# A transformer encoder block on one core: one pool of tile rings for all stages, first operands of a stage asked for within the stage before, and the last two groups of the down projection side by side

## The chip, the cores and the metric

The kernel runs on one core of a Trainium2 chip. The metric is the device time of one execution in microseconds (us); a figure for a kernel is the median of several runs. The engines have the names of the profile: PE (TensorE, matmuls), PEld (its weight loads), DVE (VectorE), ACT (ScalarE), POOL (GpSimd) and SP (SyncE, which issues the DMA transfers here). PEclk is the share of its full clock that PE was granted.

## The reference

One layer over 2048 tokens of width 1024, in fp32, and a last norm:

```python
def mixer_layer(x, ...):          # convolution heads and gated linear attention heads
    z = rms_norm(x, mix_norm) @ w_in
    ...
    return concat([y_conv, y_gla]) @ w_out
def memory_cross_attention(x, mem, ...):   # 4 heads, 256 memory tokens
    ...
def sq_relu_mlp(x, mlp_norm, w_up, w_down):
    h = rms_norm(x, mlp_norm) @ w_up       # 1024 -> 4096
    return jnp.square(jax.nn.relu(h)) @ w_down
x = x + mixer_layer(x, ...)
x = x + memory_cross_attention(x, mem, ...)
x = x + sq_relu_mlp(x, mlp_norm, w_up, w_down)
return rms_norm(x, final_norm)
```

Below, x2 is the value of x after the cross attention, held in DRAM (`x2d`, features by tokens), and zu is relu(...)², also in DRAM.

## The kernel before, in words

Every fp32 product is made of three fp32r matmuls: an operand is split in a high and a low part (`split`, L112: ACT casts the high part at L113, DVE subtracts it from the source at L114), and `mm3` (L139) accumulates high x high, high x low and low x high in PSUM. All tiles have 128 partitions. Instructions are issued per engine in program order as a scheduler lays them out; an engine whose next instruction waits holds up all that is behind it.

The stages follow each other: memory keys, input projection, convolution and linear attention (to about 860 us), output projection (to about 1100 us), cross attention in 8 blocks of 256 tokens (L918 to L947, to 1419 us), the up projection (to 2113 us) and the down projection with the final norm (to the end).

**Cross attention.** The loop over `s` keeps one block ahead: scores of block s+1, probabilities of block s (`xa_probs`), output of block s. The last block ends with `xa_last` (its matmuls stand from 1395 to 1418 us). `xa_in` loads a block and takes the sum of squares of its tokens. During the last blocks x2 of the first 1024 tokens is read back from DRAM (`prep_load`, `fold`, with the adds on POOL) for the norm of the MLP; the reciprocal square roots are laid out as `rows`. Then the pool `big` is closed (L950).

**Up projection** (pool `up`, L952). It runs for two halves `hf` of 1024 tokens; in each half over 16 pairs `f` of weight tiles. One f is a 2x2 block product done with seven products instead of eight (as in Strassen's method), each of 12 matmuls 128x512 (`product`, L1053), so 84 matmuls an f. The seven token operands of a half, X1 to X7, come from `token_side`: four quarters of x2 are loaded and normed (DVE, L1014: 4 instructions a quarter), POOL makes four sums of 128x2048 elements of them (L975 with `eng=nc.gpsimd`), and each operand is split. X1, X4 and X2 are quarters or sums that need no POOL, X5, X6, X7, X3 need a POOL sum. The seven weight operands of an f come from `weight_side(f)`: two loads of 512 KB, four DVE adds of 128x512 and splits. `weight_side(f + 1)` is asked for at the start of f. The products run in the order 1, 5, 6, 2, 7, 4, 3; their results meet in PSUM tiles px, py, pz, pw and are combined by DVE in the tiles c1, u2, c22 (L975) and squared by ACT or DVE. Product 3 is accumulated upon product 5 in pz, so it must come after the DVE add that makes c22 out of pz and c1. At f 12 of the first half the sums of squares of the second half's tokens are taken (`squares`), at f 15 its `rows`. The operands of the second half are asked for when its loop starts. Then `up` is closed (L1113).

**Down projection** (pool `dn`). 16 groups `g` of two weight tiles; `dn_load(g + 1)` (weights and the zu tiles with their splits) is asked for at the start of group g. In a group there are four blocks of 512 tokens, in each 8 feature tiles `d` of 6 matmuls; DVE adds the PSUM result to `acc` (L975), which starts as x2 and is loaded after `dn_load(0)`. In the last group each finished block has its squares taken on ACT and summed on POOL, and `final_norm` (L1144) of a block is called after the matmuls of the next one: matmuls against a column of ones, L147 on DVE, a power on POOL (L149), `to_rows` on PE (L165), 8 scales on DVE (L1151) and 8 stores. The last block is cut in two of 256 tokens.

Of the kernel before, what the change touches and what calls it, by code (L numbers as in the profile page):

```python
# [30 lines left out]
def block_kernel(ctx, tc, x, mem, wm, wv, wlg, wlog, wout, wxk, wxv, wxqT, wxo, wup, wdn,  # L31
# [3 lines left out]
    phase = ExitStack()  # L35
    big = phase.enter_context(tc.tile_pool(name="big", bufs=1))
# [3 lines left out]
    NA, NG = 25, 8  # L40
# [50 lines left out]
    rows = cpool.tile([P, 2, TB], F32, name="rows")  # L91
    nhalf = cpool.tile([P, 16], F32, name="nhalf")
# [422 lines left out]
    rmem = cpool.tile([P, NMEM], F32, name="rmem")  # L515
# [126 lines left out]

    def xa_in(s, h=None):
# [266 lines left out]

    xa_rstd(0)
# [6 lines left out]
    for s in range(NS):  # L918
        if s + 1 < NS:
# [11 lines left out]
        else:  # L931
            xa_probs(s, 0)
            xa_probs(s, 1)
            xa_last(s)
# [19 lines left out]
    def W8(*shape):

        t = up.tile([P, 2048], F32, tag="w8", name="w8", bufs=6)
        return t.rearrange("p (a b) -> p a b", a=shape[0]) if shape else t

    def C8():
        return up.tile([P, 4, TB], F32R, tag="c8", name="c8", bufs=14)  # L960

    def H8():
        return up.tile([P, 2, 1024], F32R, tag="h8", name="h8", bufs=4)

    def H4():
        return up.tile([P, 2, TB], F32R, tag="h4", name="h4", bufs=2)

    def U2():
        return up.tile([P, TB], F32, tag="u2", name="u2", bufs=6)

    def US(n):
        return up.tile([P, 16], F32, tag="us", name="us", bufs=4)[:, :n]

    def add(out, a, b, op=ALU.add, eng=nc.vector):
        eng.tensor_tensor(out=out, in0=a, in1=b, op=op)  # L975

    def quarter(b, k):

        t = W8(4, TB)
        nc.sync.dma_start(t, x2d[k * TB:(k + 1) * TB, b * TB:(b + 1) * TB].rearrange("(j p) t -> p j t", p=P))  # L980
        return t

    def squares(b):

        acc = None
        for k in range(2):
            t = quarter(b, k)
            nc.scalar.activation(t, t, AF.Square)
            add(t[:, 0:2], t[:, 0:2], t[:, 2:4], eng=nc.gpsimd)
            if acc is not None:  # L990
                add(t[:, 0:2], t[:, 0:2], acc[:, 0:2], eng=nc.gpsimd)
            acc = t
        add(acc[:, 0], acc[:, 0], acc[:, 1], eng=nc.gpsimd)
        return acc[:, 0]
# [252 lines left out]
```

## Time and profile before

| | |
|---|---|
| time, median of 3 runs | 2863.25 us (2860.94 to 2864.39) |
| the profiled execution's own time | 2863.58 us |
| its span (first to last instruction) | 2861.8 us |
| PE busy | 2688.0 us, 94% |
| PE weight loads | 2286.7 us, 80% |
| DVE busy | 1584.1 us, 55% |
| ACT busy | 844.8 us, 30% |
| POOL busy | 220.0 us, 8% |
| DMA | 108 GB/s over the span |
| mean granted PE clock | 0.97 |

The page of the profile gives busy times for each engine and cuts the span into 40 slices of 71.5 us. The trace behind it can be asked for a stretch of time (windows: busy time of each engine, the granted clock, DMA share), for an engine's instructions one after the other (timeline: start, duration, what, and in brackets the idle time just before and what ended it) and for the chain of work that ended last. An instruction written L975 is made by line 975; the tile names are those of the program.

### The profile page before, as it was taken

How to read it: one execution, taken by the hardware profiler on the slowest of the kernel's cores; microseconds unless marked ns; L12 is line 12 of the kernel's file. 1: busy time of each engine (PE TensorE's matmuls, PEld its weight loads, DVE VectorE, ACT ScalarE, POOL GpSimd, SP SyncE). 2: the span in 40 equal slices, each digit the busy share in tenths (PEclk: the TensorE clock that was granted, in tenths of full speed). 3: DMA queues.
4: the chain of work that ended last, by engine and by line, in shares of the span. 5: the costliest groups of instructions: out<-in, count | busy, mean ns of one | idle time of the engine just before them, and what ended most of it. 6: DMA issues, size and time to landing. Idle time of an engine off the chain costs nothing. (4 is left out here: it accounts for less than half of the span.)

```text
span 2861.8 us, 34708 instructions
## 1 busy us (share of the span) xinstructions
PE 2688.0 (94%) x13848; PEld 2286.7 (80%) x13848; DVE 1584.1 (55%) x2367; ACT 844.8 (30%) x1216; POOL 220.0 (8%) x157
## 2 busy tenths in 40 slices
PE   6999989988889999999869998899989999999996
PEld 6898878877777889999758877688868888888885
DVE  6413372567766544333286565856547665665655
ACT  5411162423445332222233343333322011110112
POOL 1000010302200000000220020200000000000004
PEclk9999999999999999999979998899999999999998
DMA  7412363234445441111333343333253221221203
GB/s 239 156 62 67 111 216 118 89 101 117 138 144 158 153 141 45 52 41 49 123 123 112 114 144 136 103 118 101 84 205 130 85 89 45 89 89 45 89 1 118
DMA packets 157089, 310.24 MB, mean 108 GB/s; under 512 B 14016, under 2 KB 70464, under 8 KB 151808
## 3 DMA queue, kind: packets, MB, share of 16 engines
q1 hardware_dynamic: 156928, 308.04, 32.3%
q8 instruction: 108, 1.77, 0.3%
q14 instruction: 53, 0.43, 0.1%
HBM read 219.90 MB, written 88.08 MB: 108 GB/s over the span
## 5 line engine op out<-in xcount | busy, mean ns | idle before, releaser
L1058 PE MATMUL ps<-c,h 128*128 128x512 f32 x1536 | 375.7, 400 | 49.0 <-ACT c L113 35.3
L1058 PEld LDWEIGHTS ps<-c,h 128*128 128x128 f32 x1536 | 296.4, 194 | 117.6 <-ACT c L113 37.5
L141 PE MATMUL ps<-a,a 128*128 128x512 f32 (+1 forms) x840 | 305.3, 363 | 6.7 <-DVE t L245 6.7
L142 PE MATMUL ps<-a,a 128*128 128x512 f32 (+1 forms) x840 | 304.8, 363 | 0.0
L143 PE MATMUL ps<-a,a 128*128 128x512 f32 (+1 forms) x840 | 303.7, 362 | 0.0
L1058 PE MATMUL pg<-c,h 128*128 128x512 f32 x1152 | 275.2, 392 | 6.2 <-DVE c L114 3.4
L1058 PEld LDWEIGHTS pg<-c,h 128*128 128x128 f32 x1152 | 217.4, 189 | 53.4 <-DVE c L114 4.5
L975 DVE TENSOR_TENSOR acc<-ps,acc 128x512 f32<-128x512 f32 (+1 forms) x260 | 176.5, 680 | 121.6 <-PE ps L143 121.1
L975 DVE TENSOR_TENSOR acc<-pg,acc 128x512 f32<-128x512 f32 (+1 forms) x260 | 176.6, 680 | 119.5 <-PE pg L143 117.6
L141 PE MATMUL pg<-uh,wh 128*128 128x512 f32 (+1 forms) x520 | 201.9, 389 | 11.0 <-ACT uh L113 10.2
L141 PE MATMUL ps<-uh,wh 128*128 128x512 f32 (+1 forms) x520 | 202.0, 389 | 1.0 <-DVE acc L1151 1.0
L142 PE MATMUL pg<-uh,wh 128*128 128x512 f32 (+1 forms) x520 | 201.8, 388 | 0.0
L143 PE MATMUL pg<-uh,wh 128*128 128x512 f32 (+1 forms) x520 | 201.7, 388 | 0.0
L142 PE MATMUL ps<-uh,wh 128*128 128x512 f32 (+1 forms) x520 | 201.6, 388 | 0.0
L143 PE MATMUL ps<-uh,wh 128*128 128x512 f32 (+1 forms) x520 | 201.5, 388 | 0.0
L113 ACT CAST h<-w 128x1024 fp32r<-128x1024 f32 (+1 forms) x128 | 120.7, 946 | 249.1 <-PE pg L1058 135.2
L113 ACT CAST wh<-wr 128x1024 fp32r<-128x1024 f32 x32 | 33.6, 1052 | 532.6 <-PE ps L143 503.0
L114 DVE TENSOR_TENSOR h<-w,h 128x1024 fp32r<-128x1024 f32 (+1 forms) x128 | 152.4, 1193 | 62.8 <-ACT h L113 62.8
L141 PEld LDWEIGHTS ps<-a,a 128*128 128x128 f32 x840 | 160.7, 191 | 33.0 <-DVE t L245 6.3
L143 PEld LDWEIGHTS ps<-a,a 128*128 128x128 f32 x840 | 160.8, 191 | 23.2 <-issue 0.4
L142 PEld LDWEIGHTS ps<-a,a 128*128 128x128 f32 x840 | 160.9, 192 | 22.9 <-issue 0.2
L114 DVE TENSOR_TENSOR a<-raw,a 128x1024 fp32r<-128x1024 f32 (+1 forms) x76 | 88.3, 1173 | 133.2 <-PE ps L142 73.3
(320 smaller groups left out, 5221.4 us busy)
## 6 DMA issues: line engine op xcount, KB each, us to landing
w<-in_wup SPq DMA_DIRECT2D x64, 512.0 KB, 5.1
zu<-u SPq DMA_DIRECT2D x128, 256.0 KB, 2.4
ur<-zu SPq DMA_DIRECT2D x32, 1024.0 KB, 5.9
raw<-in_wm SPq DMA_DIRECT2D x32, 512.0 KB, 4.2
wr<-in_wdn SPq DMA_DIRECT2D x32, 512.0 KB, 5.4
w<-x2d SPq DMA_DIRECT2D x12, 1024.0 KB, 6.0
a<-in_x SPq DMA_DIRECT2D x32, 256.0 KB, 6.7
gt<-zv SPq DMA_DIRECT2D x32, 256.0 KB, 3.2
```

The source lines that it names most:

```text
L113: mark["act"] = nc.scalar.copy(hi, src)
L114: nc.vector.tensor_tensor(out=lo, in0=src, in1=hi.bitcast(F32), op=ALU.subtract)
L141: nc.tensor.matmul(ps, lh, rh, start=first, stop=False)
L142: nc.tensor.matmul(ps, lh, rl, start=False, stop=False)
L143: mark["pe"] = nc.tensor.matmul(ps, ll, rh, start=False, stop=last)
L975: eng.tensor_tensor(out=out, in0=a, in1=b, op=op)
L1058: nc.tensor.matmul(ps, W[w][:, ks], X[x][:, kt], start=first and kt + w + x == 0, stop=kt == 3 and w == 1, skip_group_check=not first)
```

## The change

Seven things are changed together.

1. The pools `up` and `dn` are gone; all stages take tiles from the rings of `big`, which stays open (`a` of 128x1024 tiles grows from 25 to 28, `A4`; `g` has 8, `G4`; smaller rings `st`, `raw`, `cv`, `t2`, `gt`). An operand X now is four A4 tiles, so one half's seven operands fill all 28; those of the second half take the tiles that the products of f 15 release. In the down projection 16 A4 tiles are `acc`, and 12 hold zu operands.
2. The sums of squares for the MLP norm are taken from x2 while a block of the cross attention is still in SBUF (`sumsq`, `x2_rstd`, `x2_rows`), instead of reading x2 again.
3. The first token operands (1 and 4), their loads and norms, the POOL adds and `weight_side(0)` are asked for before `xa_last` of the last block; those of the second half at f 14 and f 15 of the first.
4. The products run in the order 1, 4, 5, 6, 2, 7, 3.
5. A POOL add of 128x2048 becomes two of 128x1024 (`both`), and weight operands other than product 1's and 2's are split in pieces of 128x512.
6. `dn_load` loads zu by halves of 1024 columns; `acc` is 16 tiles, loaded by halves.
7. The last two groups of the down projection are taken together: for each block of tokens the matmuls of both groups, then the next block. `finish` of a block (sums, power, rows, scales, stores) is laid by hand between the feature tiles of the next block on PE and DVE. The last block's squares are summed on DVE.

The core of the diff:

```diff
-    phase = ExitStack()
-    big = phase.enter_context(tc.tile_pool(name="big", bufs=1))
+    big = ctx.enter_context(tc.tile_pool(name="big", bufs=1))
-    NA, NG = 25, 8
+    NA, NG = 28, 8
...
             xa_probs(s, 1)
+            x2_rstd(s - 1)
+            sides = [token_side(0)]
+            next(sides[0])
+            X = dict([next(sides[0])])
+            W = weight_side(0, T2)
+            X.update([next(sides[0])])
             xa_last(s)
+            f_last = sumsq(live[s]["xs"])
             continue
         xa_out(s, 0)
         if s + 2 < NS:
             xa_in(s + 2)
-        else:
-            G2 = lambda: G4(F32, (P, 2, TB))
-            sq = [fold(prep_load(x2d, b, XR), G2, nc.gpsimd) for b in (0, 1)]
...
-    phase.close()
-    up = phase.enter_context(tc.tile_pool(name="up", bufs=1, reuse_waits="tile"))
...
+    def both(out, a, b, op):
+        for i in range(2):
+            add(out[i], a[i], b[i], op, nc.gpsimd)
...
+    def token_side(hf):
+        a11 = quarter(hf, 0, 0, S2())
+        a22 = quarter(hf, 1, 1, R2())
+        a21 = quarter(hf, 1, 0, S2())
+        yield None
+        yield 1, operand(a11)
+        yield 4, operand(a22)
+        s = a22
+        both(s, a21, a22, ALU.add)
+        yield 5, operand(s)
+        both(s, s, a11, ALU.subtract)
+        yield 6, operand(s)
+        both(a21, a11, a21, ALU.subtract)
+        a12 = quarter(hf, 0, 1, S2())
+        yield 2, operand(a12)
+        yield 7, operand(a21)
+        both(a12, a12, s, ALU.subtract)
+        yield 3, operand(a12)
...
-            nxt = weight_side(f + 1) if f + 1 < 16 else None
+            if f + 1 < 16:
+                nxt = weight_side(f + 1)
+            if hf == 0 and f == 14:
+                sides.append(token_side(1))
+                next(sides[1])
             product(px, W[1], x(1), True)
             nc.scalar.copy(c1, px)
+            product(pw, W[4], x(4), True)
             product(pz, W[5], x(5), True)
             product(py, W[6], x(6), True)
...
-            product(pw, W[4], x(4), True)
             add(c1, c1, pw, ALU.subtract)
             product(pz, W[3], x(3), False)
...
+            if hf == 0 and f == 15:
+                nxt = weight_side(0)
...
+    pair = [nxt, dn_load(NG_ - 1)]
+    blocks = [(0, cs) for cs in halves] + [(1, halves[0]), (1, slice(TB, TB + TH)), (1, slice(TB + TH, 2 * TB))]
+    todo = None
+    with tc.manual_schedule(engines={EngineType.PE, EngineType.DVE}):
+        for n, (c, cs) in enumerate(blocks):
+            column(*pair[0], c, cs, between=todo)
+            sq = column(*pair[1], c, cs, nc.vector if n == len(blocks) - 1 else nc.gpsimd, todo)
+            for _ in todo or ():
+                pass
+            todo = finish(c, cs, sq)
```

How the order of instructions moves is shown at three places.

DVE, in the middle of a half of the up projection, one f between its products 6 and 3. Before, `u_14724` is u2, `u_14698` is c1, `u_14755` is c22, `h` are split weight operands and `w` weight sums:

```order
L975 TENSOR_TENSOR u_14724<-pg,u_14698 128x512
L114 TENSOR_TENSOR h_14667<-w_14665,h_14667 128x1024
L114 TENSOR_TENSOR h_14668<-w_14665,h_14668 128x1024
L975 TENSOR_TENSOR w_15049<-w_15046 128x512
L975 TENSOR_TENSOR u_14698<-pg,u_14698 128x512
L975 TENSOR_TENSOR w_15049<-w_15046,w_15049 128x512
L975 TENSOR_TENSOR u_14755<-ps,u_14698 128x512
```

After, `t_15232` is u2, `t_15194` is c1, `t_15263` is c22, `g` are split weight operands and `gt` weight sums:

```order
L924 TENSOR_TENSOR t_15232<-pg,t_15194 128x512
L114 TENSOR_TENSOR g_15153<-gt,g_15152 128x512 x2
L924 TENSOR_TENSOR gt<-cv,raw 128x512
L924 TENSOR_TENSOR gt<-cv,gt 128x512
L114 TENSOR_TENSOR g_15155<-gt,g_15154 128x512 x2
L924 TENSOR_TENSOR gt<-gt,raw 128x512
L924 TENSOR_TENSOR gt<-cv 128x512
L924 TENSOR_TENSOR t_15194<-pg,t_15194 128x512
L114 TENSOR_TENSOR g_15291<-raw,g_15290 128x1024
L924 TENSOR_TENSOR t_15263<-ps,t_15194 128x512
```

All four weight sums, four splits of 128x512 and one of 128x1024 now stand between u2 and c22.

POOL, from the end of the cross attention to the first half's last operand. Before (`w` are the quarters and sums of the up projection; the row of L149 makes both `rows`):

```order
L149 TENSOR_TENSOR sm<-sm,nhalf 128x4 x2
L975 TENSOR_TENSOR w_11998<-w_11986,w_11992 128x2048
L975 TENSOR_TENSOR w_11986<-w_11962,w_11986 128x2048
L975 TENSOR_TENSOR w_11998<-w_11998,w_11962 128x2048
L975 TENSOR_TENSOR w_12035<-w_12035,w_11998 128x2048
```

After (`st`, `raw`, `cv` are the quarters and sums; the two rows of L149 are the powers of `x2_rstd` for block 6 and of the last block's sums, which follow `xa_last`):

```order
L924 TENSOR_TENSOR raw<-st,raw 128x1024
L924 TENSOR_TENSOR st<-st 128x1024
L924 TENSOR_TENSOR cv<-st,cv 128x1024
L924 TENSOR_TENSOR st<-st 128x1024
L149 TENSOR_TENSOR sm<-sm,nhalf 128x2
L924 TENSOR_TENSOR raw<-raw,st 128x1024
L924 TENSOR_TENSOR cv<-cv,st 128x1024
L149 TENSOR_TENSOR sm<-sm,nhalf 128x2
L924 TENSOR_TENSOR st<-st,raw 128x1024
L924 TENSOR_TENSOR st<-st,cv 128x1024
```

A half has eight adds instead of four, and six of them stand ahead of the power that follows `xa_last`.

PE, where the up projection ends. Before, the last product 3 (L1058 on `ps`), then the first matmuls of the down projection (L141 to L143 on `uh`, `wh`):

```order
L1058 MATMUL ps<-c_14259,h_15949 128x512 x2
L1058 MATMUL ps<-c_14260,h_15949 128x512
L1058 MATMUL ps<-c_14259,h_15949 128x512
L141 MATMUL pg<-uh,wh 128x512
L141 MATMUL ps<-uh,wh 128x512
```

After, the end of product 7 (L1009 on `pg`), eight matmuls of the down projection, and product 3 (L1009 on `ps`):

```order
L1009 MATMUL pg<-a_14533,g_16413 128x512
L141 MATMUL pg<-a_16661,g_16656 128x512
L142 MATMUL pg<-a_16662,g_16656 128x512
L143 MATMUL pg<-a_16661,g_16657 128x512
L141 MATMUL pg<-a_16673,g_16668 128x512
L142 MATMUL pg<-a_16674,g_16668 128x512
L143 MATMUL pg<-a_16673,g_16669 128x512
L141 MATMUL ps<-a_16661,g_16656 128x512
L142 MATMUL ps<-a_16662,g_16656 128x512
L1009 MATMUL ps<-a_14563,gt 128x512
```

The down projection's first matmuls thus stand ahead of the up projection's last product.

More of the change, by code (lines that the diff above doesn't have):

```diff
@@ L512, in gla_out @@
         return attn, outp, fin
-    rmem = cpool.tile([P, NMEM], F32, name="rmem")
+    rmem = rows[:, 0, :NMEM]
     memT = []
@@ L909, in block_kernel, with add, kts, operand @@
     wA = [load_w(row(zA, kt)) if kt < 6 else load_st(row(zA, kt)) for kt in range(KT)]
+    def add(out, a, b, op=ALU.add, eng=nc.vector):
+        eng.tensor_tensor(out=out, in0=a, in1=b, op=op)
+    def kts(t):
+        return [t[j // 2][:, (j % 2) * TB:(j % 2 + 1) * TB] for j in range(4)]
+    def operand(src):
+        c = [A4(F32R) for _ in range(4)]
+        for i in range(2):
+            split(src[i], c[i], c[2 + i])
+        return kts(c[:2]), kts(c[2:])
+    def S2():
+        t = ST(F32, (P, 2, 1024))
+        return [t[:, i] for i in range(2)]
@@ new lines, in product, with sq_relu @@
+    def product(ps, W, X, first):
+        for kt in range(4):
+            ks = slice(kt * P, (kt + 1) * P)
+            for w, x in ((0, 0), (0, 1), (1, 0)):
+                nc.tensor.matmul(ps, W[w][:, ks], X[x][kt], start=first and kt + w + x == 0,
+                                 stop=kt == 3 and w == 1, skip_group_check=not first)
+    def sq_relu(t, src, f, b):
+        nc.scalar.activation(t, src, AF.Relu)
+        nc.scalar.activation(t, t, AF.Square)
+        nc.sync.dma_start(zu[f * P:(f + 1) * P, b * TB:(b + 1) * TB], t)
@@ L968, in U2 @@
[L968 to L994, printed above, removed]
@@ L1053, in product @@
-    def product(ps, W, X, first):
-        for kt in range(4):
-            ks = slice(kt * P, (kt + 1) * P)
-            for w, x in ((0, 0), (0, 1), (1, 0)):
-                nc.tensor.matmul(ps, W[w][:, ks], X[x][:, kt], start=first and kt + w + x == 0,
-                                 stop=kt == 3 and w == 1, skip_group_check=not first)
-    def sq_relu(t, src, f, b):
-        nc.scalar.activation(t, src, AF.Relu)
-        nc.scalar.activation(t, t, AF.Square)
-        nc.sync.dma_start(zu[f * P:(f + 1) * P, b * TB:(b + 1) * TB], t)
@@ new lines, in finish @@
+    def finish(c, cs, sq):
+        for _ in range(3):
+            yield
+        rc = final_sums(sq, cs.stop - cs.start, PS)
+        yield
+        yield
+        r = to_rows(rc, PG)
+        for d in range(KT):
+            final_scale(c, cs, r, d)
+            yield
+    NG_ = FF // P // G
+    halves = [slice(0, TB), slice(TB, 2 * TB)]
+    for g in range(NG_ - 2):
+        (us, ws), nxt = nxt, dn_load(g + 1)
+        for c in range(2):
+            for cs in halves:
+                column(us, ws, c, cs)
@@ new lines, in block_kernel @@
+    pair = [nxt, dn_load(NG_ - 1)]
[8 more added lines that the diff above has]
+            todo = finish(c, cs, sq)
+        for _ in todo:
+            pass
```

258 lines of the change are left out of this document (111 added, 147 removed).

## The prediction

> **What bounds the kernel now.** I read the page first:
>
> ```profile
> span 2861.8 us, 34708 instructions
> PE 2688.0 (94%) x13848; PEld 2286.7 (80%) x13848; DVE 1584.1 (55%) x2367; ACT 844.8 (30%) x1216; POOL 220.0 (8%) x157
> PE   6999989988889999999869998899989999999996
> PEclk9999999999999999999979998899999999999998
> ```
>
> PE is busy 94% of the span, so nothing but PE's own holes can be won. In its row the dips from the middle on are slices 21 (a 6, with the clock at 7), 25 and 26 (8, clock 8), 30 (8) and the last (6, clock 8). They are the openings of the up projection's two halves, that of the down projection, and the end of the kernel. Sums by windows size them; the columns are busy time of PE, PEld, DVE, ACT, POOL, then granted clock, DMA share and GB/s:
>
> ```profile
> 1150.00:1395.00 245.00, 243.96 (x1607) 222.97 (x1606) 90.35 (x208) 63.26 (x150) 22.49 (x15) 1.00 0.18 57
> 1395.00:1419.00 24.00, 23.47 (x196) 23.21 (x193) 3.79 (x10) 1.23 (x3) 0.00 (x0) 1.00 0.03 9
> 1419.00:1441.00 22.00, 0.47 (x1) 0.29 (x1) 15.83 (x22) 7.12 (x7) 0.00 (x0) 0.58 0.90 325
> 1441.00:1480.00 39.00, 25.52 (x79) 18.14 (x79) 32.13 (x18) 14.82 (x11) 20.57 (x4) 0.75 0.10 34
> 1771.00:1784.00 13.00, 7.09 (x35) 6.51 (x34) 7.13 (x13) 3.54 (x4) 2.87 (x2) 0.62 0.64 234
> 1784.00:1828.00 44.00, 29.33 (x88) 21.14 (x89) 36.62 (x22) 14.86 (x12) 20.60 (x4) 0.73 0.09 30
> 2113.00:2124.00 11.00, 0.79 (x3) 0.40 (x2) 3.03 (x4) 2.54 (x3) 0.00 (x0) 0.61 0.80 285
> 2124.00:2131.00 7.00, 6.96 (x20) 5.03 (x20) 5.44 (x5) 3.44 (x4) 0.00 (x0) 0.63 1.01 421
> 2131.00:2780.00 649.00, 649.00 (x2865) 537.39 (x2864) 421.17 (x570) 87.24 (x90) 0.00 (x0) 1.00 0.23 83
> ```
>
> The row 2131:2780 gives the price of one 128x512 matmul at full clock: 649 / 2865 = 0.2265 us. The timeline of PE gives the same (one f is 84 matmuls, from 1516.77 to 1535.81, 19.04 us or 0.2267 each) and shows the holes:
>
> ```profile
> 1440.53 0.79 PE L1058 MATMUL ps<-c,h 128*128 128x512 f32 x1 [22.06 <-ACT c L113]
> 1452.91 2.50 PE L1058 MATMUL ps<-c,h 128*128 128x512 f32 x5 [5.58 <-ACT c L113]
> 1516.77 8.32 PE L1058 MATMUL ps<-c,h 128*128 128x512 f32 x36
> 1535.81 8.32 PE L1058 MATMUL ps<-c,h 128*128 128x512 f32 x36
> 1690.85 10.08 PE L1058 MATMUL ps<-c,h 128*128 128x512 f32 x36 [2.56 <-DVE u L975]
> 2110.51 2.88 PE L1058 MATMUL ps<-c,h 128*128 128x512 f32 x12
> 2123.60 0.79 PE L141 MATMUL pg<-uh,wh 128*128 128x512 f32 x1 [10.21 <-ACT uh L113]
> 2127.16 0.63 PE L142 MATMUL pg<-uh,wh 128*128 128x512 f32 x1
> 2127.59 0.63 PE L143 MATMUL pg<-uh,wh 128*128 128x512 f32 x1
> ```
>
> What each hole holds beyond its matmuls:
>
> - Opening 1, 1419 to 1480: 61 us for 80 matmuls, 61 - 80 x 0.2267 = **42.9**. First 22 us of nothing (loads, norms, first split: the pool had just been closed), then waits for operands.
> - A stall at 1690: 2.56 idle, and the 36 matmuls behind it take 10.08 instead of 8.32: **4.3**. It stands where the second half's squares are taken.
> - Opening 2, 1771 to 1828: 57 us for 88 products of 0.2267 and 0.4 us of small ones: 57 - 20.4 = **36.6**.
> - Opening 3, 2113.2 (2110.51 + 12 x 0.2267) to 2131: 17.8 us for 23 matmuls, 17.8 - 5.2 = **12.6**.
> - The down projection from 2131 to the end of the span: 730.8 us. All of it is 16 x 192 x 0.2267 = 696.4, of which 23 matmuls are counted above: 730.8 - 691.2 = **39.6**, nearly all after 2780.
>
> That is 136.0 us in five places, and the change touches all five.
>
> **Why an operand takes so long to make.** In opening 1 POOL and DVE stand like this:
>
> ```profile
> 1440.51 2.29 DVE L114 TENSOR_TENSOR c<-w,c 128x2048 fp32r<-128x2048 f32 x1
> 1452.89 4.79 DVE L114 TENSOR_TENSOR c<-w,c 128x2048 fp32r<-128x2048 f32 x1 [6.78 <-ACT c L113]
> 1457.60 7.02 DVE L1014 SCALAR_TENSOR_TENSOR w<-w,vec,rows 128x512 f32<-128x512 f32 x4
> 1550.70 1.22 DVE L114 TENSOR_TENSOR h<-w,h 128x1024 fp32r<-128x1024 f32 x1 [1.49 <-ACT h L113]
> ```
>
> ```profile
> 1446.42 9.11 POOL L975 TENSOR_TENSOR w<-w,w 128x2048 f32<-128x2048 f32 x2 [52.51 <-DVE w L1014]
> 1457.76 4.99 POOL L975 TENSOR_TENSOR w<-w,w 128x2048 f32<-128x2048 f32 x1 [2.23 <-DVE c L114]
> ```
>
> The last DVE row, from the middle of the half, is a split of 128x1024: 1.22. The split of 128x2048 takes 2.29 us alone and 4.79 when it starts at 1452.89 within a POOL add, and the four norms that run into POOL's add at 1457.76 take 7.02. So a POOL add and a DVE instruction with two SBUF inputs do not run together: the later one waits. [...] What the change can do about it is only to put the adds elsewhere and to halve their length.
>
> **The change, part by part.**
>
> *Opening 1.* The 22 us go: loads, norms and the operands of products 1 and 4 lie within the cross attention, where DVE has room (3.79 of 24 us in 1395:1419). Cover: `xa_last`, 23 us of matmuls in that row. But two costs take their place. First, the new work stands on ACT, DVE and POOL ahead of the last block's probabilities; a weight load that waits for its ring slot, two casts and a POOL lock of half an add (4.5 us for 128x2048 by 9.11 / 2, so 2.3) delay `xa_last` by about 3 to 5. Second, products 1 and 4 of f 0 and product 1 of f 1 give PE only 36 x 0.2267 = 8.2 us before X5, X6, X2, X7 are needed, each of which wants a POOL add or a norm behind POOL, casts and two splits of about 1.15. Before, from the first product (1440.5) to full rate (1480) 39.5 us held 18 of matmuls, 21 lost; six of eight adds now lie earlier, so I take 13 of these and 2 to 3 of half clock after a stall. Left: 4 + 13 + 2.5 = 19.5 of 42.9, **gain 23**. Bounds: the 22 less 5 of `xa_last`'s delay and 5 of new waits, 12; all hidden but 4 of that delay and 2.9 of clock, 36.
>
> *Stall at 1690.* The reads and POOL adds behind it are gone: -4.3. `x2_rows` and `x2_rstd` in its place cost some small matmuls, about 1.3. **Gain 3** (0 to 4.3).
>
> *Opening 2.* The 13 us of `rows` at its head go (done at f 12), and loads and norms are done during f 14. But all 28 A4 tiles hold the first half's operands: X1 of the second can be split only when product 1 of f 15 is over, and so on in turn, and X5 needs four tiles behind product 5. Each split is behind POOL's add and behind product 7's results on DVE's one queue, in 19 us of f 15. DVE has in that f its usual work of 10.7 us (seven combining steps and four weight sums of 0.6, splits of 1.1 + 5 x 0.6), 14 splits of 128x1024 at 1.15 are 16 us more and POOL's adds 8 x 2.3 = 18 lock against these. That can't end in 19 us: 10.7 + 16 + part of 18 is 30 to 40. I take 20 left of 36.6, **gain 16** (8, the 13 less 5 of new waits, to 30, where only 6.6 is left).
>
> *Opening 3.* `dn_load(0)` takes tiles that product 1 and 4 of the last f release, 14 us before its end, and eight matmuls of the down projection stand ahead of product 3. `acc` needs its first tile after 1.4 us and is loaded behind product 5's release. About 0.6 left, **gain 12** (8 to 12.6).
>
> *Tail.* The end now, and the sums and rows on PE from the chain:
>
> ```profile
> 2842.65 4.74 POOL L975 TENSOR_TENSOR q<-q 128x256 f32<-128x256 f32 x6 [6.30 <-ACT q L1175]
> 2847.35 0.71 POOL L149 TENSOR_TENSOR ds<-ds,nhalf 128x2 f32<-128x2 f32 x1
> 2852.81 0.71 POOL L149 TENSOR_TENSOR ds<-ds,nhalf 128x2 f32<-128x2 f32 x1 [4.06 <-DVE ds L147]
> 2843.30 0.42 DVE L975 TENSOR_TENSOR acc<-ps,acc 128x256 f32<-128x256 f32 x1
> 2854.90 3.22 DVE L1151 SCALAR_TENSOR_TENSOR acc<-acc,vec,ps 128x256 f32<-128x256 f32 x8 [2.17 <-PE ps L165]
> ```
>
> ```profile
> 2834.91 1.37 PE ps L165 x8
> 2853.57 1.23 PE ps L165 x4
> ```
>
> Blocks finish one 512-block of matmuls apart now, 96 x 0.2267 = 21.8 us, instead of 10.9, so a block's POOL sums and scales (13 us) fit under the next block. After the last matmul: an add, a square and two sums on DVE (0.42 each), sums on PE and L147 0.5, power 0.71, rows 1.2, scales 3.22, and 3.7 from the last scale (2858.1) to the span's end: 11. Before it, final sums and rows of four blocks on PE, 1.4 each by the row of L165 at 2834.91, 5.6, and stalls between blocks about 4. Left 20.6 of 39.6, **gain 19** (13 to 24).
>
> *Steady state.* This goes the other way. Before, product 3 began 0.4 us after c22 and never waited:
>
> ```profile
> 1546.95 0.69 DVE L975 TENSOR_TENSOR u<-pg,u 128x512 f32<-128x512 f32 x1 [6.20 <-issue]
> 1549.61 1.05 ACT L113 CAST h<-w 128x1024 fp32r<-128x1024 f32 x1 [1.66 <-PE ps L1058]
> 1553.17 0.68 DVE L975 TENSOR_TENSOR w<-w,w 128x512 f32<-128x512 f32 x1
> 1553.77 0.68 DVE L975 TENSOR_TENSOR u<-ps,u 128x512 f32<-128x512 f32 x1
> 1554.85 5.38 PE L1058 MATMUL ps<-c,h 128*128 128x512 f32 x23
> ```
>
> Now product 4 no longer stands between 7 and 3; product 1 of the next f and one matmul do, so 37 x 0.2267 = 8.4 us lie between the end of product 6 and product 3. DVE has behind u2 eleven more instructions up to c22 itself, 0.60 apart (1.13 behind the split of 128x1024), and the cast before that split (1.05) waits for product 7, which ends 5.4 us in. u2 starts 0.26 in: 0.26 + 9 x 0.6 = 5.7, with waits for two casts 6.0, c1 to 6.6, the split to 7.8, c22 to 8.5. That is 0.1 late; with the error of such a sum 0 to 0.25 each f, for 30 f's **a loss of 4** (0 to 8). The queue waits only for itself; what is behind it is DVE's next f, with 8 us to spare.
>
> *Ahead of the up projection.* Squares of x2 (2 casts' worth of ACT, about 3 us of DVE a block) lie beside PE (DVE 90 of 245 us there), and three more A4 tiles let loads start earlier: 0 (-4 to +4).
>
> **Sum.** 23 + 3 + 16 + 12 + 19 - 4 = 69. The profiled execution took 2863.58, 0.33 above the median and 1.8 more than its span, so about 2863.5 - 69 = **2794**.
>
> The half clock after a stall is in the traces: PEclk 0.58 to 0.75 in the openings, and 0.43 us a matmul. [...]
>
> **Rivals.**
>
> (a) *The openings only move.* POOL's lock and the chain add, cast, split, matmul stay as they are, and the added work delays `xa_last` and f 15 by what is saved. For it: POOL's 20.6 us in each opening are the same elements; the A4 ring is full. Against: 22 us of opening 1 wait for loads and norms alone. Then only opening 3, the tail, the stall and the loss count: 12 + 19 + 3 - 4 = 30, 2833. Chance 0.15.
>
> (b) *The openings vanish.* Operands are ready in time but for some 5 us each: gains 37 and 31, and no loss in the steady state: 37 + 31 + 3 + 12 + 19 = 102, 2761. For it: DVE is busy 57% in the steady f (10.7 of 19). Against: f 15's sum above. Chance 0.15.
>
> (c) *Slower: product 3 waits on DVE's queue in every f.* The place is c22, eleventh behind u2. If one of the casts before it waits for a later product than I read (the `g` ring has eight tiles for six an f), c22 comes late by a cast and the splits behind it: product 7 instead of product 2 for the second pair of splits makes 5.7, cast 0.6, two splits 1.2, two sums 1.2, c1 0.6, split 1.1 and c22 0.7, together 11.1, which is 2.7 late, 30 x 2.7 = 81 lost instead of 4: 2863.5 - 73 + 81 = 2872. It decides from 73 / 30 = 2.4 us an f. Against: the tiles come free in turn, and the product that I read is 2, one before 7. Chance 0.04, a further 0.02 for a loss that just eats the gain.
>
> (d) *The scheduler undoes it*: the prefetches are placed behind `xa_last`'s work anyway. The order shows them ahead, so this counts within (a).
>
> The forecast has 0.64. 0.2% of the time, 5.7 us, is about what a measurement of this kernel can tell from no change. Range: the forecast's terms in quadrature (12, 12, 6, 4, 4) give about 19, or 25 for eight times in ten; up to 2832 it takes in most of (a), down to 2764 part of (b): 2764 to 2832. Faster 0.94, same 0.02, slower 0.04.
>
> **What would show it.** Right: the first 22 us hole gone with X1's product right behind `xa_last`; PE waits of 1 to 6 us for ACT or DVE in openings 1 and 2, POOL's adds beside long splits; no 10 us hole before the down projection; some 20 us less at the end; gaps of 0.1 to 0.2 before product 3 in each f. Wrong: `xa_last` later by more than 8, opening 2 over 30 or under 8, or a pitch of an f over 19.3.

## The result, and the profile after

The changed kernel takes **2796.05 us** (median of four runs, 2792.35 to 2800.03); the kernel before, run beside it, 2862.58. The ratio is 0.9768, interval 0.9751 to 0.9785: 2.3% faster, 66.5 us. The prediction was 2794.0 in 2764 to 2832. The profiled execution took 2798.06 us with a span of 2795.9, 65.9 less than the span before. One execution of a later repeat of this kernel (e9 below) took 6807.44 us; e9's median counts it (2789.53 without it), its ratio does not. The page of the profile:

```profile
span 2795.9 us, 35187 instructions
PE 2677.4 (96%) x13896; PEld 2281.7 (82%) x13896; DVE 1613.2 (58%) x2504; ACT 859.2 (31%) x1298; POOL 190.4 (7%) x146
PE   7999989988889999999989999899999999999998
PEclk8999999999999999999999999899999999999999
```

PE is busy 10.6 us less although it has 48 matmuls more, since fewer of them run at half clock: the mean granted clock is 0.98 instead of 0.97, and over opening 1, as defined below, 0.95 (1402.2 to 1501.92) instead of 0.85 (1395.1 to 1516.77). The other 55 us are idle time that went. Slice 21 went from 6 to 8 and its clock from 7 to 9, one 8 is left of slices 25 and 26, slice 30 is a 9, and the last slice went from 6 to 8.

*The openings.* PE's timeline around the end of `xa_last` (L1009 is the product's line now, `a` the token operand, `g` or `gt` the weight operand), then product 3 in f 2, f 11 to f 14 and the second f of the second half:

```profile
1432.32 2.91 PE L1009 MATMUL ps<-a,g 128*128 128x512 f32 x12
1435.40 5.73 PE L1009 MATMUL ps<-a,g 128*128 128x512 f32 x24 [0.17 <-ACT a L113]
1445.20 0.61 PE L157 MATMUL pg<-vec,t 128*128 128x1 f32 x4 [4.07 <-DVE t L651]
1460.57 1.66 PE L1009 MATMUL pg<-a,g 128*128 128x512 f32 x6 [1.35 <-DVE a L114]
1463.90 1.89 PE L1009 MATMUL pg<-a,g 128*128 128x512 f32 x7 [1.67 <-DVE a L114]
...
1501.92 3.03 PE L1009 MATMUL ps<-a,gt 128*128 128x512 f32 x12
...
1674.43 3.00 PE L1009 MATMUL ps<-a,gt 128*128 128x512 f32 x12
1693.58 2.99 PE L1009 MATMUL ps<-a,gt 128*128 128x512 f32 x12
1714.54 3.03 PE L1009 MATMUL ps<-a,gt 128*128 128x512 f32 x12
1733.73 3.00 PE L1009 MATMUL ps<-a,gt 128*128 128x512 f32 x12
...
1810.02 3.00 PE L1009 MATMUL ps<-a,gt 128*128 128x512 f32 x12
```

The hole of 22 us is gone: product 1 starts where `xa_last` ends. To compare kernels I measure both openings in one way. Opening 1 runs from the last transpose of the probabilities to product 3 of f 2, opening 2 from product 3 of f 14 to product 3 of the second half's second f; the matmuls between (at 0.12 and 0.2267 us) are subtracted. Before, the transposes ended at 1395.1 and product 3 of f 2 began at 1516.77: 121.7 - 192 x 0.12 - 240 x 0.2267 = 44.2 beyond the matmuls. After, 1402.2 to 1501.92, with 253 instead of 240 matmuls, is 99.7 - 80.4 = 19.3. Opening 2 was 94.2 - 57.1 = 37.1 and is 1810.02 - 1733.73 - 57.1 = 19.2. In the steady part nine f's lie between 1501.92 and 1674.43: 19.17 each, where it was 19.04. The `rows` of the second half are 16 small matmuls on PE just ahead of 1693.58; the two f's around them, from 1674.43 to 1714.54, take 40.11, which is 1.8 more than two steady ones.

*What holds PE in opening 2.* In order: POOL's sums (L924), DVE's queue, PE.

```profile
1740.21 3.38 POOL L924 TENSOR_TENSOR raw<-st,raw 128x1024 f32<-128x1024 f32 x1 [277.45 <-DVE a L114]
1743.67 2.40 POOL L924 TENSOR_TENSOR st<-st 128x1024 f32<-128x1024 f32 x1
1746.03 3.32 POOL L924 TENSOR_TENSOR cv<-st,cv 128x1024 f32<-128x1024 f32 x1
```

```profile
1744.71 2.44 DVE L114 TENSOR_TENSOR a<-raw,a 128x1024 fp32r<-128x1024 f32 x1 [3.37 <-ACT a L113]
1750.47 2.40 DVE L114 TENSOR_TENSOR a<-cv,a 128x1024 fp32r<-128x1024 f32 x1 [3.31 <-ACT a L113]
1752.79 0.68 DVE L924 TENSOR_TENSOR t<-pg,t 128x512 f32<-128x512 f32 x1
1753.39 5.05 DVE L114 TENSOR_TENSOR g<-gt,g 128x512 fp32r<-128x512 f32 x2
```

```profile
1753.52 4.41 PE L1009 MATMUL pg<-a,g 128*128 128x512 f32 x12 [6.15 <-DVE t L924]
1764.38 5.49 PE L1009 MATMUL ps<-a,gt 128*128 128x512 f32 x12 [3.05 <-DVE t L924]
1784.27 4.38 PE L1009 MATMUL pg<-a,g 128*128 128x512 f32 x12 [3.55 <-DVE t L924]
```

This is one chain, read from the bottom. PE waits 6.15 us for the combining step at 1752.79, which takes 0.68 and would have been possible long before; but it is queued on DVE behind the split at 1750.47, which waits 3.31 for ACT's cast, and the cast waits for POOL's sum that ends at 1749.4. The splits take 2.4 instead of 1.22, and two of 128x512 take 5.05 where 1.3 is usual, while POOL's adds run on to 1757.90. In these rows a split and an add of POOL hold each other up. The split begun at 1744.71, within POOL's add of 1743.67 to 1746.07, takes 2.44 and ends 1.08 us after that add; POOL's next add, begun at 1746.03 within this split, takes 3.32 instead of 2.40. The combining step at 1752.79, which has one input in PSUM, keeps its 0.68 although a POOL add runs from 1751.75 to 1755.10. What these rows show is called the lock below, as in the prediction. PE's three waits are 12.75 us, and the 12 matmuls behind each take 1.5, 2.6 and 1.5 more than the 2.88 of full clock: 18.4 of the 19.2.

*Opening 3 and the tail.* PE at the start of the down projection, then DVE at the end:

```profile
2072.60 2.88 PE L1009 MATMUL pg<-a,g 128*128 128x512 f32 x12
2075.32 0.39 PE L141 MATMUL pg<-a,g 128*128 128x512 f32 x1
2077.13 2.90 PE L1009 MATMUL ps<-a,gt 128*128 128x512 f32 x12
2079.87 0.39 PE L143 MATMUL ps<-a,g 128*128 128x512 f32 x1
```

```profile
2787.06 0.16 DVE L147 TENSOR_SCALAR sm<-ps 128x2 f32<-128x2 f32 x1 [0.70 <-PE ps L1138]
2789.31 3.22 DVE L1143 SCALAR_TENSOR_TENSOR a<-a,vec,pg 128x256 f32<-128x256 f32 x8 [2.09 <-PE pg L165]
```

The first matmul of the down projection follows product 7 (L1009 on `pg`) without a gap, where 12.6 us stood. From 2075.32 to the end are 720.6 us; without product 3 (2.7) and the 696.4 of matmuls 21.5 are left of 39.6.

### The profile page after: what moved, and what is told of

It reads as the page before. It is cut to its first block, busy times and chain, and to the rows that moved or that the text cites. A ratio compares the mean times of both kernels' runs of the same rounds, so it can differ in the third digit from the quotient of the medians.

```text
span 2795.9 us, 35187 instructions
## 1 busy us (share of the span) xinstructions
PE 2677.4 (96%) x13896; PEld 2281.7 (82%) x13896; DVE 1613.2 (58%) x2504; ACT 859.2 (31%) x1298; POOL 190.4 (7%) x146
## 5 line engine op out<-in xcount | busy, mean ns | idle before, releaser
L141 PE MATMUL ps<-a,a 128*128 128x512 f32 (+1 forms) x840 | 307.1, 366 | 6.8 <-DVE t L245 6.8
L143 PE MATMUL ps<-a,a 128*128 128x512 f32 (+1 forms) x840 | 306.5, 365 | 0.0
L1009 PE MATMUL pg<-a,g 128*128 128x512 f32 x1152 | 287.0, 394 | 13.1 <-DVE t L924 9.7
L1009 PE MATMUL ps<-a,g 128*128 128x512 f32 x1152 | 277.5, 389 | 0.2 <-ACT a L113 0.2
L1009 PEld LDWEIGHTS pg<-a,g 128*128 128x128 f32 x1152 | 219.3, 191 | 61.4 <-DVE t L924 6.6
L141 PE MATMUL ps<-a,g 128*128 128x512 f32 (+1 forms) x672 | 260.0, 387 | 0.0
L143 PE MATMUL ps<-a,g 128*128 128x512 f32 (+1 forms) x672 | 258.3, 384 | 0.0
L142 PE MATMUL ps<-a,g 128*128 128x512 f32 (+1 forms) x672 | 258.2, 384 | 0.0
L1009 PEld LDWEIGHTS ps<-a,g 128*128 128x128 f32 x1152 | 216.0, 188 | 45.4 <-ACT a L113 0.6
L924 DVE TENSOR_TENSOR a<-ps,a 128x512 f32<-128x512 f32 (+1 forms) x264 | 178.0, 674 | 121.4 <-PE ps L143 120.0
L924 DVE TENSOR_TENSOR a<-pg,a 128x512 f32<-128x512 f32 (+1 forms) x264 | 177.9, 674 | 115.7 <-PE pg L143 115.6
L113 ACT CAST g<-raw 128x1024 fp32r<-128x1024 f32 (+3 forms) x118 | 114.9, 983 | 360.7 <-issue 237.6
L141 PE MATMUL pg<-a,g 128*128 128x512 f32 (+1 forms) x528 | 202.7, 384 | 0.0
L143 PE MATMUL pg<-a,g 128*128 128x512 f32 (+1 forms) x528 | 202.0, 383 | 0.0
L142 PE MATMUL pg<-a,g 128*128 128x512 f32 (+1 forms) x528 | 202.0, 383 | 0.0
L141 PEld LDWEIGHTS ps<-a,a 128*128 128x128 f32 x840 | 162.8, 194 | 32.3 <-DVE t L245 4.8
L143 PEld LDWEIGHTS ps<-a,a 128*128 128x128 f32 x840 | 162.8, 194 | 23.1
L114 DVE TENSOR_TENSOR g<-raw,g 128x1024 fp32r<-128x1024 f32 (+3 forms) x118 | 137.4, 1173 | 29.8 <-ACT g L113 28.3
```

What stands on the lines that cost most here:

```text
L113: mark["act"] = nc.scalar.copy(hi, src)
L114: nc.vector.tensor_tensor(out=lo, in0=src, in1=hi.bitcast(F32), op=ALU.subtract)
L141: nc.tensor.matmul(ps, lh, rh, start=first, stop=False)
L142: nc.tensor.matmul(ps, lh, rl, start=False, stop=False)
L143: mark["pe"] = nc.tensor.matmul(ps, ll, rh, start=False, stop=last)
L1009: nc.tensor.matmul(ps, W[w][:, ks], X[x][kt], start=first and kt + w + x == 0, stop=kt == 3 and w == 1, skip_group_check=not first)
```

## The experiments

What was in dispute after the result: why 19 us are left in each opening. The first theory is the prediction's: in opening 2 DVE has more work than time, and the ring of `A4` tiles is full. The rival: POOL's token sums, through the lock with DVE and as a link of the chain. Besides, it was open which part of the change (one pool, the requests, the pair of groups) brought what. The measured numbers of all kernels stand here; openings are us beyond the matmuls, as defined above, and "down" is from the up projection's last product 3 to the end of the span.

| kernel | median us | ratio to before (interval) | opening 1 | opening 2 | down |
|---|---|---|---|---|---|
| before | 2862.58 | 1 | 44.2 | 37.1 | |
| after | 2796.05 | 0.9768 (0.9751 to 0.9785) | 19.3 | 19.2 | 718.8 |
| e9, after again | 2792.93 | 0.9755 (0.9738 to 0.9772) | 19.5 | 19.2 | 718.8 |
| e1, no requests ahead | 2805.22 | 0.9805 (0.9791 to 0.982) | 34.7 | 17.3 | 718.3 |
| e2, sums on DVE | 2762.25 | 0.9654 (0.9639 to 0.9667) | 6.3 | 2.7 | |
| e3, no pair of groups | 2800.0 | 0.9788 (0.9772 to 0.9804) | 18.8 | 19.3 | 727.0 |
| e4, weights of the output projection later | 2790.44 | 0.9756 (0.974 to 0.9773) | 18.8 | 19.3 | 718.8 |
| e5, before, sums on DVE | 2839.61 | 0.9933 (0.9915 to 0.9951) | 34.7 | 22.5 | |
| e6, after, `s` in its own tiles | 2791.13 | 0.9761 (0.9746 to 0.9775) | 22.0 | 16.4 | |
| e7, e2 with before's order of products | 2765.29 | 0.9666 (0.9648 to 0.9685) | 7.7 | 6.2 | |
| e8, e2 with idle work on POOL | 2792.34 | 0.9765 (0.9743 to 0.9787) | 26.3 | 17.9 | |
| e10, e2 and e4 | 2757.6 | 0.9634 (0.9617 to 0.965) | 6.3 | 2.7 | |
| e11, e2 and e1 | 2772.06 | 0.9689 (0.9675 to 0.9704) | 17.9 | 2.7 | |

In opening 2 of e2, e8, e10 and e11 one matmul more than 252 lies between the two product 3, and its 0.2 us are still in the figures; in e7 there are five more, and their 1.1 us are taken off. The ratios hold each kernel against runs of the kernel before that were made beside it.

**e1: the requests back at the start of each half, one pool kept.** The blocks that call `token_side` and `weight_side` within the cross attention and at f 14 and 15 are taken out; instead:

```diff
+        if hf == 0:
+            sides = []
+        X = {}
+        sides.append(token_side(hf))
+        next(sides[hf])
+        X.update([next(sides[hf])])
+        W = weight_side(0)
```

> The changed kernel, with the requests put back to the start of each half: token operands and first weight operands of a half are asked for when its loop begins, as before the change, but still in the one pool. Theory A (the one pool does the work, the requests little: the order already lays loads and norms ahead of the last block's matmuls): the last block starts some 4 to 6 us earlier, the first product of the up projection some 3 to 5 us later behind it, opening 2 within 2 us of the changed kernel; 2791 to 2801. Theory B (the requests bring the gain of the openings, 23 and 16 us): openings of 36 to 43 and 30 to 37 us again, 2815 to 2835.

Measured 2805.22, 9 us above after. Product 3 of f 2, of f 14 and of the second f of half 2:

```profile
1511.70 3.02 PE L1009 MATMUL ps<-a,gt 128*128 128x512 f32 x12
...
1743.46 3.00 PE L1009 MATMUL ps<-a,gt 128*128 128x512 f32 x12
...
1817.83 3.02 PE L1009 MATMUL ps<-a,gt 128*128 128x512 f32 x12
```

The transposes ended at 1396.6. So opening 1 is 115.1 - 80.4 = 34.7, 15 more than after; opening 2 is 74.4 - 57.1 = 17.3, no more than after. (The spans differ by 7.3 only, since e1's transposes ended 5.6 earlier; see e9.) In the second opening the requests bring nothing: what shortened it from 37.1 lies in the rest of the rewrite, which stays in e1. Its largest part can be read from the kernel before, where the `rows` of the second half and X1's first cast held up PE from 1771.5 to 1784.1, 12.6 us with 32 small matmuls; now the `rows` are made at f 12. The sums in halves and product 4 right behind product 1 were not tried one by one. In the first opening the requests bring 15, though not through loads and norms: all but the last quarter's norms end by 1381.4 in e1 as well. What stands behind the last block's work there are the casts and splits of X1 and X4, and POOL's sums behind them: X1 is split at 1425.2 instead of 1390.1, and POOL's first sum starts at 1434.7 instead of 1394.1. The hole of 22 us does not come back; PE waits 1.1 us for X1. Whether that is due to the one pool or to the norm's sums, which are now taken beforehand, no run separates.

**e2: the eight token sums of a half on DVE.** One word:

```diff
-            add(out[i], a[i], b[i], op, nc.gpsimd)
+            add(out[i], a[i], b[i], op)
```

> The changed kernel, with the token sums (eight adds of 128x1024 in each half) on DVE instead of POOL. Theory A (what is left of the openings is POOL's chain and its lock on DVE: 2.4 to 3.4 us an add on POOL, splits of 2.4 instead of 1.2 beside them): each opening 3 to 6 us shorter, 2784 to 2790. Theory B (DVE's own load is the bound there: 10.7 us of one f and 16 of splits): the adds come on top, 9 us each, 2804 to 2814.

Measured 2762.25, 34 us below after and far below both theories. The openings are 13.0 and 16.5 us shorter, 29.5 together, where theory A had 3 to 6 each; in the profiles most of the rest lies ahead of them, as e2's transposes ended 7.5 earlier (see e9). Product 3 at the same three places, and below it the sums by windows over opening 2 of after and of e2 (PE, PEld, DVE, ACT, POOL busy, then PEclk, DMA share, GB/s):

```profile
1481.35 3.00 PE L1009 MATMUL ps<-a,gt 128*128 128x512 f32 x12
...
1713.11 3.00 PE L1009 MATMUL ps<-a,gt 128*128 128x512 f32 x12
...
1772.87 2.91 PE L1009 MATMUL ps<-a,gt 128*128 128x512 f32 x12
```

```profile
1733.73:1810.02 76.29, 63.55 (x254) 51.04 (x253) 62.16 (x70) 32.80 (x47) 24.18 (x8) 0.89 0.36 111
```

```profile
1713.11:1772.87 59.76, 58.32 (x254) 47.19 (x254) 57.53 (x74) 33.28 (x47) 0.00 (x0) 1.00 0.43 137
```

DVE now has the eight sums as well, 8 x 1.22 = 9.8 us, and is busy 57.5 of 59.8 us; yet opening 2 falls from 19.2 to 2.7 and PE's clock stays at 1. So DVE's work was not too much for the time, and the full `A4` ring did not bind either: the ring is the same. The second half's 14 splits lie between 1713.0 and 1762.1 in e2, over two and a half f's and not within f 15 alone. The eight sums took POOL 24.2 us, and they made DVE's other instructions longer, as its groups in the same windows show, after and then e2:

```profile
L114 DVE TENSOR_TENSOR g<-gt,g 128x512 fp32r<-128x512 f32 x12 | 13.6, 1177 | 0.0
L114 DVE TENSOR_TENSOR a<-st,a 128x1024 fp32r<-128x1024 f32 x8 | 11.9, 1495 | 0.0
```

```profile
L114 DVE TENSOR_TENSOR a<-st,a 128x1024 fp32r<-128x1024 f32 x8 | 9.6, 1219 | 0.0
L114 DVE TENSOR_TENSOR g<-gt,g 128x512 fp32r<-128x512 f32 x12 | 7.6, 686 | 0.0
```

This leaves two readings of the gain: the lock, or only the faster sums in the chain. e8 tells them apart.

**e5: the kernel before with its four sums of 128x2048 on DVE** (`eng=nc.gpsimd` dropped in four lines).

> The kernel before, with one edit: its four token sums of 128x2048 in each half on DVE instead of POOL. Theory A (the lock between POOL and DVE also held up the openings of the kernel before, beside loads and the closed pool): each opening some 8 to 12 us shorter, 2838 to 2846. Theory B (there the loads and norms bound the openings, and the sums only mattered once these were hidden): within 5 us of 2860.

Measured 2839.61, 19.6 us below the runs of before that were made beside it (2859.23). Both openings shrink, by 9.5 and 14.6 us, but the hole ahead of the first product stays:

```profile
1441.21 0.80 PE L1058 MATMUL ps<-c,h 128*128 128x512 f32 x1 [22.27 <-ACT c L113]
```

POOL's sums were thus a cost of their own in the kernel before, beside the 22 us that the change removes, and the change left them on POOL.

**e8: e2, and POOL adds a constant to the high parts of operands 5, 6, 7 and 3,** into a scratch tile that nobody reads: 16 pieces of 128x512 a half. No operand depends on POOL's work. In opening 2 it takes more of POOL's time than the sums did, 30.1 us against 24.2, so that it shows what the lock can do, and not the exact share that it had in the change.

```diff
+            if d is not None:
+                for j in range(2):
+                    add(d, cst[:, :TB], c[i][:, j * TB:(j + 1) * TB].bitcast(F32), eng=nc.gpsimd)
```

> The kernel with the sums on DVE, and beside each of the operands 5, 6, 7 and 3 POOL adds a constant to the operand's high part, in four pieces of 128x512, into a scratch tile that nobody reads (16 pieces a half, some 20 us of POOL; no work of the reference is left out). Nothing waits for these, so only the lock between POOL and DVE can cost. Theory A (the lock is what cost the openings): 10 to 25 us slower than 2762. Theory B (the chain through the slower POOL adds is what cost): within 4 us of 2762.

Measured 2792.34: 30 of e2's 34 us are lost again. One POOL piece alone in opening 1 and the 16 of opening 2, then DVE's groups in opening 2, and a wait of PE (L1013 here is L1009 elsewhere):

```profile
1438.50 1.28 POOL L924 TENSOR_TENSOR gt<-cst,a 128x512 f32<-128x512 f32 x1
...
1761.98 31.26 POOL L924 TENSOR_TENSOR gt<-cst,a 128x512 f32<-128x512 f32 x16 [296.85 <-DVE g L114]
```

```profile
L114 DVE TENSOR_TENSOR a<-st,a 128x1024 fp32r<-128x1024 f32 x8 | 14.8, 1876 | 0.0
L114 DVE TENSOR_TENSOR g<-gt,g 128x512 fp32r<-128x512 f32 x12 | 9.8, 864 | 0.0
L959 DVE SCALAR_TENSOR_TENSOR st<-st,vec,rows 128x512 f32<-128x512 f32 x4 | 5.9, 1511 | 2.0 <-DMA st<-x2d 2.0
```

```profile
1769.83 2.93 PE L1013 MATMUL ps<-a,g 128*128 128x512 f32 x6 [3.99 <-DVE a L114]
```

No wait in opening 2 names POOL, and in opening 1 only two of DVE do, 1.0 us in all, for the power of the norm's sums and not for these pieces; PE waits for DVE's splits, which take 1.88 instead of 1.22 us in the mean. The spans differ by 30.2 us: opening 1 takes 20.0 and opening 2 15.2 more, while the work ahead of them ends 5.0 earlier. So the lock alone, with no dependence on POOL, costs the openings 35.2 us, more than the 29.5 that e2 won there. How the 29.5 divide between the lock and the slower chain through POOL's sums is not shown. The rows show both sides paying: POOL's 16 pieces take 30.1 / 16 = 1.88 instead of 1.28, too.

**e6: the first sum in tiles of its own.** In after, `s` overwrites `a22`, so POOL's first sum waits for the split of X4 (the 277 us at 1740.21 end with that split).

```diff
-        s = a22
+        s = R2()
```

> The changed kernel, sums still on POOL, but the first sum written to tiles of its own instead of over the operand of product 4, so that POOL need not wait until that operand is split into tiles that product 4 of f 15 frees. Theory A (what cost 16 us in opening 2 is when POOL's chain may start): opening 2 some 6 to 9 us shorter, 2787 to 2791. Theory B (it is the length of POOL's chain and the lock, wherever it starts): opening 2 within 3 us of 18.9, 2793 to 2799.

Measured 2791.13, within the intervals of after. POOL's first sum starts 0.6 us before product 3 of f 14 (at 1727.8) instead of 6.5 after it (at 1740.2), but opening 2 gets only 2.8 us shorter, and opening 1 gets 2.7 longer. So it is not the start of POOL's chain that holds opening 2.

**e3: the last two groups of the down projection one after the other** (the first through all four half-blocks, then the last, with `finish` still between its matmuls).

```diff
+    for c in range(2):
+        for cs in halves:
+            column(*pair[0], c, cs)
...
-            column(*pair[0], c, cs, between=todo)
```

> The changed kernel, with the last two groups of the down projection one after the other again; each block's sums, rows and scales still lie between the feature tiles of the next block, which now has 10.9 us of matmuls instead of 21.8. Theory A (the gain at the end, 18 us, comes from the pair): 12 to 18 us slower, 2808 to 2814. Theory B (it comes from the interleaving and the sums on DVE, the pair only costs buffers): within 4 us, 2792 to 2800.

Measured 2800.0 as a median, 4 us above after, not to be told apart by the intervals; but the stage itself is clear. Down takes 2797.0 - 2070.04 = 727.0 instead of 718.8, and PE waits for the power of a block's sums. Over the whole execution this is 12.2 us in six waits, 3.7 in three after; within the down projection it is 9.5 in four and 1.0 in one:

```profile
PE pg L165 <- POOL sm L149: 12.2, 6, 3.1
```

```profile
PE pg L165 <- POOL sm L149: 3.7, 3, 1.4
```

The pair is worth 8 of the 18 us that the tail became shorter. That the spans differ by 1.1 us only comes from the start of the execution: the transposes ended 6.6 us earlier than in the profile of after (see e9).

**e9: the changed kernel once more.**

> The changed kernel itself once more, beside the next two. Theory A (the wait of 4.0 us at the first sums of squares of the cross attention, which its profile showed, belongs to that one execution): the first transposes of the cross attention's probabilities start at 1078 to 1081 us instead of 1085.3, the median is 2790 to 2798. Theory B (it belongs to the change): 1084 to 1086 again.

Measured 2792.93. The transposes of the cross attention in the profile of after, and in this one:

```profile
L712 PE MATMUL pg<-cst,t x128: 271/273/302, 1085.3 to 1402.2; 128*128 128x128 f32 x128
```

```profile
L712 PE MATMUL pg<-cst,t x128: 271/272/302, 1076.7 to 1393.6; 128*128 128x128 f32 x128
```

The span is 8.5 us shorter, 2787.4, and all of it lies ahead of the first transpose, 8.6 us; the openings and the down projection are the same to 0.2. So the profile shown of after is an execution in which the early stages took long, and the 7 us by which its transposes end later than before's are no effect of the change. Over the profiles of the kernels made from the changed one the transposes end anywhere from 1389.7 (e8) to 1402.2. What in those stages varies I have not found.

**e4: six of the eight weight tiles of the output projection loaded later** (behind its last sum of the stage before), against a wait of PE at L157 near 1037 which is 4.0 us in the profile of after.

```diff
-            wO = [load_w(row(zO, kt), T=A4 if kt < 6 else G4) for kt in range(KT)]
+            wO = [load_w(row(zO, kt), T=A4 if kt < 6 else G4) for kt in range(2)]
+            with behind("y"):
+                wO += [load_w(row(zO, kt), T=A4 if kt < 6 else G4) for kt in range(2, KT)]
```

> The changed kernel, with all but two of the eight loads and splits of the cross attention's output weights laid behind the last add of the output projection. Theory A (the larger ring let a third weight split stand ahead of those adds on DVE, and PE waits 4.0 us for them and runs some us at half clock): 5 to 6 us faster, 2790 to 2791, with no wait at the first sums of squares. Theory B (the 6 us come from elsewhere, or the later weights are then missed): within 2 us of 2796 or slower.

Measured 2790.44, the number of theory A. The wait is gone, but in other executions of the kernel without the edit it is only 1.1 to 1.8, and the ratios 0.9756 and 0.9768 or 0.9755 do not differ. No effect can be shown.

**e7: e2 with before's order of products (1, 5, 6, 2, 7, 4, 3), operands in that order, `s` in its own tiles.** It tests the loss in the steady part.

> The kernel with the sums on DVE, and the order of products of the kernel before (1, 5, 6, 2, 7, 4, 3), operands made in that order too, the first sum in tiles of its own. Theory A (product 3 waits 0.13 us in each f for the sum c22, since a split of 128x1024 stands before it on DVE; with product 4 between 7 and 3 it need not): an f takes 19.04 instead of 19.17 us, and the openings lose some 1 to 3 us each, 2756 to 2763. Theory B (the longer f has another cause): 19.17 us an f still.

Measured 2765.29, no better than e2. Nine f's apart, product 3 shows the pitch, and a wait of opening 2 where the gain went:

```profile
1503.70 2.88 PE L1009 MATMUL ps<-a,gt 128*128 128x512 f32 x12
...
1675.06 2.88 PE L1009 MATMUL ps<-a,gt 128*128 128x512 f32 x12
...
1750.86 0.51 PE L1009 MATMUL ps<-a,g 128*128 128x512 f32 x1 [3.10 <-ACT a L113]
```

171.36 / 9 = 19.04: the loss of the steady part is due to the new order. But opening 2 has 6.2 instead of 2.7 left, and opening 1 7.7 instead of 6.3: product 4 no longer stands behind product 1, where its 12 matmuls gave the operands behind it 2.7 us. That reason is argued, not tried by itself. What 28 f's by 0.13 bring, 3.6, is paid in the two openings.

**e10: e2 and e4 together.**

> The kernel with the sums on DVE, and the output weights of the cross attention laid behind the last add of the output projection. Theory A (that weight split in front of the adds costs in some executions): 2756 to 2761 and a smaller spread. Theory B (it costs nothing measurable): within 3 us of 2762.

Measured 2757.6, the fastest kernel here: 0.9634 (0.9617 to 0.965). Against e2's 0.9654 the intervals overlap, so e4's part stays undecided.

**e11: e2 and e1 together,** the requests without the lock.

> The kernel with the sums on DVE, and the operands and first weights of a half asked for when its loop begins. Theory A (the request is worth the time in which X1 and X4 are split behind the last block, about 5 to 9 us, and the rest of the 15 us that it was worth with sums on POOL was the lock): 2766 to 2772. Theory B (it is worth the same 15 us without the lock): 2775 to 2780.

Measured 2772.06. Opening 1 is 17.9 instead of 6.3 us, opening 2 is 2.7 as in e2. The requests are thus worth 12 us in opening 1 (15 with the sums on POOL, e1) and nothing in opening 2, with the lock or without it.

## Why the prediction was right

By its own steps, predicted gain and measured one (us):

| step | predicted | measured | from |
|---|---|---|---|
| opening 1 | 23 | 24.9 | 44.2 to 19.3 |
| stall at 1690 | 3 | 2.5 | 4.3 to 40.11 - 2 x 19.17 |
| opening 2 | 16 | 17.9 | 37.1 to 19.2 |
| opening 3 | 12 | 12.6 | no gap left |
| tail | 19 | 18.1 | 39.6 to 21.5 |
| steady state | -4 | -3.6 | 28 x (19.17 - 19.04) |
| ahead of the up projection | 0 | -7.1 | 1395.1 to 1402.2, that execution alone |
| sum | 69 | 65.3 | the spans differ by 65.9 |

- *Opening 1* went as laid out: of the 19.3 us left, 6.8 are the delay of `xa_last` within its block (30.1 us from the last transpose to product 1, 23.3 before), where 3 to 5 were expected, and the rest new waits and half clock. POOL's sums, which the prediction charged here with their lock, are the larger part: with the sums on DVE (e2) 13.0 of the 19.3 go, 4.3 of them from the delay of `xa_last`. One wait was not foreseen: at 1445.20 PE stood 4.07 us for four small matmuls of block 7's sums, which only the second half needs; on PE's queue they stand ahead of 24 matmuls that run as soon as these four are done. In e2 the same wait is 0.82.
- *`xa_last` later by more than 8* was named as a sign against the forecast, and it did end 13.9 us later. 7.1 of these come from the early stages, and e9 shows that they are not the change's; 6.8 are. The sign was put down without a fixed start to count from.
- *Opening 2* has the predicted size, but the step that gave it is wrong in its main reason. The prediction added DVE's 10.7 and 16 us to part of POOL's 18 and said that this can't end in 19 us. e2 gives DVE 9.8 us more and opening 2 is nearly gone. What holds it is the third item of that sum: the adds on POOL, by the lock (e8) and as a link ahead of ACT's casts, behind which DVE's queue stood idle for 3.37 and 3.31 us. Nor did DVE's work have to end within f 15: in e2 the splits take two and a half f's and PE hardly waits. That 20 was taken and 19.2 came is so far luck.
- *The requests* (opening 2: "loads and norms are done during f 14") count for nothing there: without them the scheduler places loads and norms as early by itself. The norms of the second half begin 40.3 us ahead of product 3 of f 14 in e1 and 40.3 in after. No pool was closed at this place before the change either; what kept the norms back there were the `rows`, made only from 1771 on.
- *The tail*: 8 of the 18 are the pair's (e3); that the other 10 come from `finish` between the last matmuls was not tried by itself.
- *The steady state* lost what was worked out, and for that reason: with the old order the pitch is 19.04 again (e7).
- *Half clock*: the waits of 1.35 and 1.67 us in opening 1 cost only their length. But the 24 matmuls behind the wait of 4.07, at 1445.67, take 7.31 instead of 5.60, so 1.7 of the 2.5 us that the prediction's sum had for half clock did come. Around the second of the short waits the sums by windows, from 1462 to 1475, have PEclk (behind POOL's column) at 1.00:

```profile
1462.00:1475.00 13.00, 11.05 (x47) 8.64 (x47) 12.37 (x16) 5.59 (x10) 0.76 (x1) 1.00 0.80 257
```

  Each wait of 3.05 to 6.15 in opening 2, however, is followed by slow matmuls, 4.38 to 5.49 for twelve instead of 2.88, and the slowest twelve follow the shortest of these waits, 3.05. A row of opening 1 of e8 has a wait of only 1.80 and slow matmuls behind it, 4.56 for twelve, so the length of the one wait just before does not settle the clock here:

```profile
1469.87 4.56 PE L1013 MATMUL pg<-a,g 128*128 128x512 f32 x12 [1.80 <-DVE t L924]
```

- *Rival (a)*, openings that only move, is out: 24.9 and 17.9 were won. *Rival (c)*, product 3 late by 2.7 in each f, is out: 0.13. *Rival (b)*, openings that vanish, did not come with the change, but its price was right: 2761 was given for it, and e2, which is the change without POOL's sums, takes 2762.25. That the two numbers are so close is partly chance: the rival had gains of 37 and 31 and no loss in the steady part, and e2 has 37.9 and 34.4 and loses 3.6 in the steady part.

## What to carry to other kernels

Before an elementwise sum goes to POOL to relieve DVE, look at what DVE does at that time: here its splits, with two SBUF inputs, took 2.4 us beside POOL's sums instead of 1.22, and a sum of 1.22 us on DVE was cheaper than one of 2.35 to 3.38 us on POOL, even with DVE busy 96% of opening 2 (e2). When a hole stands between two stages, first see what the scheduler does by itself once one pool is kept and the norm's sums are taken beforehand, and ask for operands early only where their casts and splits would otherwise queue behind the last block. Here the two were changed together, and the hole of 22 us went with them (e1). When the size of a term comes out right, still test its reason: here the wrong reason (too much work on DVE) would have spoken against the one edit that brought another 34 us.

## What the runs showed of the hardware that was not expected

- Work on POOL that nobody waits for cost the kernel 30 us of 2762 (e8), and both engines paid: POOL 1.88 us instead of 1.28 for a piece, DVE 1.88 instead of 1.22 for a split, in the mean of eight.
- The same program's profiled executions began the transposes of the cross attention at 1085.3 and at 1076.7, with everything behind them alike to 0.2 us.
